# Seeding PSUM banks from ScalarE in the halved products of two feed-forward networks

## The chip, the core and the metric

The kernel runs on one core of a Trainium2 chip. A core has a matrix engine (TensorE, PE in the profile, its weight loads PEld), two engines for elementwise work (VectorE, DVE; ScalarE, ACT), a general engine (GpSimd, POOL) and a queue that issues transfers (SyncE, SP). They run beside each other and wait for each other through semaphores. TensorE writes only to PSUM, an on-chip memory used here as eight banks of 128 x 512 float32. The metric is the time on the device in microseconds (us), as the median of several executions; lower is better.

## The reference

One layer of a decoder on 512 tokens of 1024 features: a feed-forward network at half weight, a mixing stage (two kinds of attention, with gates), and a second feed-forward network at half weight. The change touches the two networks alone:

```python
def swiglu_ffn(x, g, w_gate, w_up, w_down):
    h = rms_norm(x, g)
    return (jax.nn.silu(h @ w_gate) * (h @ w_up)) @ w_down
```

`w_gate` and `w_up` are 1024 x 2816, that is 22 blocks of 128 columns, and `w_down` is 2816 x 1024. All is float32.

## The kernel before

**Numbers in two parts.** TensorE multiplies a rounded float32 format. Every operand is therefore split into a rounded part (`h`, `wh`, `ah`) and the remainder (`l`, `wl`, `al`), and each product is three matmuls: rounded by rounded, and the two mixed ones (`mm3`, lines 141 to 143). For weights, `split_w` casts on ScalarE (line 112) and subtracts on VectorE (line 117). For activations, `split_act` casts on ScalarE (line 212); the remainder comes either from a ScalarE negation (line 214) and a transfer issued by GpSimd that adds to its target (line 215), or, for the last pair of a group, from a VectorE difference (line 217).

**A network.** The 22 blocks are worked through in four groups: blocks 0 to 3 plainly, then three groups of six. After each group eight down steps (`run_down`) multiply the group's activations by its rows of `w_down` and add to x (line 419). The first two down steps put off the blocks that were finished last: each first does the others, and only then are the last two done, block 2q+1 ahead of block 2q.

**Pairs.** In the groups of six, blocks go in pairs (`pair_steps`), three pairs to a group, nine to a network, 18 in all. Gate and up of two blocks are a 2 x 2 product of halved matrices: features are halved, and tokens are halved to 256 columns. With Winograd's variant of Strassen's scheme it takes seven products of quarters instead of eight. The weights' quarters are a, b, c, d, with the sums s1 = c + d, s2 = s1 + a, s3 = c + a, s4 = s2 + b made on VectorE; the moving operands b1, b2, ta, tb are the quarters of the input and their sums, made once per network. A product is 24 matmuls (two halves for gate and up, four slices of features, three parts) into one bank. A bank can go on accumulating later, so several products are added up there; the banks A, B and C hold such sums, and what remains to be added is done by VectorE as it reads a bank out into `gu1` or `gu2`. `finish` then does Silu on ScalarE, the product with up on VectorE, and `split_act`.

**What sets the order.** TensorE's order is the order of the program. It runs a list of steps; ahead of step i, `look_ahead` emits the splits of weights up to step i+2 and the loads up to step i+6. There are three buffers for split weights, so the cast for step i+2 waits until TensorE has read the weights of step i-1. Raw quarters lie in five buffers; a step's last argument names those that come free after its split. The other engines' order is set by a planner, which runs the program against its own estimate of times, with dependencies and buffers. PSUM's eight banks are shared out by tag: three `acc`, two `s`, two `pt`, one `pv`. Before the change A, B and C are all `acc`; the down steps use `acc` too.

Of the kernel before, what the change touches and what calls it, by code (L numbers as in the profile page):

```python
# [11 lines left out]
F32 = mybir.dt.float32  # L12
F32R = mybir.dt.float32r
AF = mybir.ActivationFunctionType
OP = mybir.AluOpType
# [3 lines left out]
P = 128  # L19
T = 512  # L20
# [26 lines left out]
HT = T // 2  # L47
# [4 lines left out]
def tile_hybrid_layer(ctx: ExitStack, tc: tile.TileContext, a: dict):  # L52
    nc = tc.nc
    V, S, G, PE = nc.vector, nc.scalar, nc.gpsimd, nc.tensor
# [7 lines left out]
    psum = ctx.enter_context(tc.tile_pool(name="psum", bufs=1, space=PSUM))  # L62

    def acc_tile(name):
        return psum.tile([P, T], F32, tag="acc", bufs=3, name=name)

    def tmp_tile(name):
        return tmp.tile([P, T], F32, tag="t", name=name)
# [40 lines left out]
    def split_w(raw, f=1024, adding=False):  # L109
        wh = wpool.tile([P, 1088], F32R, tag="wh", name="wh")  # L110
        wl = wpool.tile([P, 1088], F32R, tag="wl", name="wl")
        S.copy(wh[:, :f], raw[:, :f])  # L112
        if adding:
            S.mul(wl[:, :f], wh[:, :f].bitcast(F32), -1.0)
            G.dma_start(wl[:, :f], raw[:, :f], accum_op=OP.add)
        else:
            V.tensor_sub(wl[:, :f], raw[:, :f], wh[:, :f].bitcast(F32))  # L117
        return wh[:, :1024], wl[:, :1024]
# [74 lines left out]
    def ffn(n, nxt, parts=lambda d: [slice(0, T)]):  # L193
        wg, wu, wp, wd = (a[f"w_{nm}{n}"] for nm in ("gate", "up", "pair", "down"))
        gi = 0 if n == 1 else 2
        with tc.tile_pool(name=f"ffn{n}", bufs=1) as ap, tc.tile_pool(name=f"halves{n}", bufs=1) as hp:
# [67 lines left out]
            def moving(nm, half):  # L264
                h, l = ops[nm]
                sl = slice(half * HT, half * HT + HT)
                return (h, l) if nm == "b1" else (h[:, :, sl], l[:, :, sl])
# [47 lines left out]
            def pair_steps(q, last):  # L315

                t, raw = {}, {}  # L320

                def view(ps):
                    return ps.rearrange("p (m t) -> p m t", m=2)

                def product(bank, w, b, start):
                    wh, wl = (z.rearrange("p (m k c) -> p m k c", m=2, k=HK) for z in w)
                    for m in range(2):
                        for k in range(HK):
                            mm3(bank[:, m * HT:(m + 1) * HT], wh[:, m, k], wl[:, m, k], b[0][:, k], b[1][:, k],
                                start and m == 0 and k == 0, m == 1 and k == HK - 1, skip_group_check=not start)  # L330

                def finish(f, gu):
                    S.activation(gu[:, 0], gu[:, 0], AF.Silu)
                    V.tensor_mul(gu[:, 1], gu[:, 1], gu[:, 0])
                    split_act(f, gu[:, 1], not last)

                def gu_tile():
                    return stream(2 + next(gu_at), F32, "gu").rearrange("p (m t) -> p m t", m=2)

                def split_a():  # L340
                    t["s1"] = stream(0, F32, "s1")
                    V.tensor_add(t["s1"], raw["c"][0], raw["d"][0])
                    return split_w(raw["a"][0])

                def split_s2():
                    t["s2"] = stream(1, F32, "s2")
                    V.tensor_add(t["s2"], t["s1"], raw["a"][0])
                    return split_w(t["s2"])

                def split_s3():  # L350
                    V.tensor_add(raw["c"][0], raw["c"][0], raw["a"][0])
                    return split_w(raw["c"][0])

                def split_s4():
                    V.tensor_add(t["s2"], t["s2"], raw["b"][0])
                    return split_w(t["s2"])

                def run_a(w):
                    t["A"] = acc_tile("pA")
                    product(t["A"], w, moving("b1", 0), True)  # L360
                    t["c1"] = tmp_tile("c1")
                    S.copy(t["c1"], t["A"])

                def run_s2(w):
                    t["B"] = acc_tile("pB")
                    product(t["B"], w, moving("tb", 0), True)
                    t["u2"] = tmp_tile("u2")
                    V.tensor_add(t["u2"], t["B"], t["c1"])

                def run_s1(w):  # L370
                    t["C"] = acc_tile("pC")
                    product(t["C"], w, moving("ta", 0), True)

                def run_s3(w):
                    product(t["B"], w, moving("ta", 1), False)
                    u3 = tmp_tile("u3")
                    V.tensor_add(u3, t["B"], t["c1"])
                    t["gu1"], t["gu2"] = gu_tile(), gu_tile()
                    V.scalar_tensor_tensor(t["gu2"][:, :, HT:], view(t["C"]), -1.0, view(u3), op0=OP.mult, op1=OP.subtract)

                def run_b(w):
                    product(t["A"], w, moving("b2", 0), False)
                    S.copy(t["gu1"][:, :, :HT], view(t["A"]))

                def run_d(w):
                    product(t["B"], w, moving("tb", 1), False)
                    V.scalar_tensor_tensor(t["gu2"][:, :, :HT], view(t["B"]), -1.0, view(t["c1"]), op0=OP.mult, op1=OP.subtract)
                    finish(2 * q + 1, t["gu2"])

                def run_s4(w):  # L390
                    product(t["C"], w, moving("b2", 1), False)
                    V.tensor_add(t["gu1"][:, :, HT:], view(t["C"]), view(t["u2"]))
                    finish(2 * q, t["gu1"])

                load = {z: (z, 0, wp[q - PLAIN // 2, i]) for i, z in enumerate("abcd")}
                return [Step(raw, [load["c"], load["d"], load["a"]], split_a, run_a),
                        Step(raw, [], split_s2, run_s2),
                        Step(raw, [load["b"]], lambda: split_w(t["s1"]), run_s1),
                        Step(raw, [], split_s3, run_s3, "ac"),
                        Step(raw, [], lambda: split_w(raw["b"][0]), run_b),  # L400
                        Step(raw, [], lambda: split_w(raw["d"][0]), run_d, "d"),
                        Step(raw, [], split_s4, run_s4, "b")]

            def run_down(d, lo, hi, held={}):

# [87 lines left out]
    with tc.tile_pool(name="begin", bufs=1) as bp, tc.manual_schedule(  # L493
# [3 lines left out]
        for d in range(KD):  # L497
            for dst, src, at in zip(first, ("w_gate1", "w_up1"), ({0: (0, 2), 2: (2, 8)}, {1: (0, 4), 4: (4, 8)})):
                if d in at:
                    lo, hi = at[d]  # L500
                    w = load_w(a[src][0][:, lo:hi], hi - lo, P, bp.tile([P, 1024], F32, name=f"raw{d}"))
# [18 lines left out]
    with (tc.tile_pool(name="mix", bufs=1) as mp, ExitStack() as att_ctx,  # L520
# [4 lines left out]
        tn, fv, iq, pA, ga, gb = {}, {}, [], [], [], []  # L525
# [246 lines left out]
        ps = transposed(lambda t: sd[1][:, t].rearrange("p a d -> p (a d)"), "ps_ik")  # L772
# [74 lines left out]
        for h in range(H):  # L847
# [3 lines left out]
            for i in range(1, NT):  # L851
                n = P * (i + 1)
                prod.run(FILL_IX)
                ps = psum.tile([P, T], F32, tag="s" if (h * 3 + i) % 2 else "pt", bufs=2, name="ps_ix")
# [156 lines left out]
        for g in range(2 * H):  # L1011
            q, k, bias = nq, nk, nb
# [31 lines left out]
        with tc.tile_pool(name="late", bufs=1) as lp:  # L1044
# [9 lines left out]
            ps = fm_product(load_w(a["w_gb"][7], KD, P), "ps_gb")  # L1054
# [6 lines left out]
            for d in range(KD):  # L1061
                wh, wl = load_w(a["w_bb"][d], 4, P)
                ps = acc_tile("ps_bb")
# [10 lines left out]
            for d in range(KD):  # L1074
                wh, wl = load_w(a["w_out"][d], KD, P)
                ps = acc_tile("ps_out")
# [86 lines left out]
```

## Time and profile before

| what | value |
| --- | --- |
| median of three executions | 1090.2 us (1090.1 to 1090.91) |
| the profiled execution: span from first to last instruction | 1087.8 us |
| TensorE matmuls, busy | 1071.0 us, 98% of the span |
| TensorE weight loads, busy | 963.3 us, 89% |
| VectorE busy | 791.2 us, 73% |
| ScalarE busy | 570.6 us, 52% |
| GpSimd busy | 197.6 us, 18% |
| read from memory | 104.94 MB |

Of the profiled execution the page gives the span; its time as the median counts it is not listed by itself, and the median lies 2.4 us above the span. A row of a group reads: line, engine, operation, output <- inputs, shapes, count, then busy time in us, the mean in ns of one, and the idle time of the engine just before, with what ended it. A row in order of time begins with start and duration in us. `x512` is a full bank, and one step's weights are `128x1024`. Matmuls overlap in the array, so the duration of one (279 ns for 256 columns) is longer than the distance between two.

### The profile page before, as it was taken

How to read it: one execution, taken by the hardware profiler on the slowest of the kernel's cores; microseconds unless marked ns; L12 is line 12 of the kernel's file. 1: busy time of each engine (PE TensorE's matmuls, PEld its weight loads, DVE VectorE, ACT ScalarE, POOL GpSimd, SP SyncE). 2: the span in 40 equal slices, each digit the busy share in tenths (PEclk: the TensorE clock that was granted, in tenths of full speed). 3: DMA queues.
4: the chain of work that ended last, by engine and by line, in shares of the span. 5: the costliest groups of instructions: out<-in, count | busy, mean ns of one | idle time of the engine just before them, and what ended most of it. 6: DMA issues, size and time to landing. Idle time of an engine off the chain costs nothing.

```text
span 1087.8 us, 17784 instructions
## 1 busy us (share of the span) xinstructions
PE 1071.0 (98%) x6808; PEld 963.3 (89%) x6808; DVE 791.2 (73%) x1286; ACT 570.6 (52%) x916; POOL 197.6 (18%) x265
## 2 busy tenths in 40 slices
PE   8999999999999999999999999999999999999998
PEld 6889989998998889999878788788889989989997
DVE  5888767856967579976776765954888758766963
ACT  6635533633555676467766656543635624533550
POOL 1100000100000014367786562000100000000000
PEclk9999999999999999999999999999999999999999
DMA  7554433443442258733323321533544442533441
GB/s 225 134 155 124 110 117 116 112 121 104 125 122 83 84 126 185 207 105 99 87 59 105 123 74 49 165 97 97 126 136 131 125 118 93 136 104 110 126 113 72
DMA packets 45444, 127.87 MB, mean 118 GB/s; under 512 B 5544, under 2 KB 5928, under 8 KB 45360
## 3 DMA queue, kind: packets, MB, share of 16 engines
q1 hardware_dynamic: 38880, 110.22, 33.1%
q0 software_dynamic: 6336, 16.26, 8.2%
q8 instruction: 54, 0.88, 0.3%
q10 hardware_dynamic: 144, 0.26, 0.1%
q14 instruction: 30, 0.25, 0.1%
HBM read 104.94 MB, written 3.42 MB: 100 GB/s over the span
## 4 chain that ended last, share of the span: by engine, by line
PE 53%; DVE 5%; ACT 3%; POOL 3%; issue 2%; DMA 0%; DVEq 0%; POOLq 0%; ACTq 0%
PE pd L142 4%; PE pd L143 4%; PE pd L141 4%; PE ps_f L141 3%; PE ps_f L142 3%; PE ps_f L143 3%; PE pB L142 2%; PE pB L141 2%; PE pB L143 2%; PE ps_t L141 2%; PE ps_t L142 2%; PE ps_t L143 2%; PE pC L142 2%; PE pA L142 2%; PE pA L141 2%
## 5 line engine op out<-in xcount | busy, mean ns | idle before, releaser
L142 PE MATMUL pd<-al,wh 128*128 128x512 f32 (+1 forms) x358 | 138.3, 386 | 1.0 <-DVE al L217 1.0
L141 PE MATMUL pd<-ah,wh 128*128 128x512 f32 (+1 forms) x358 | 138.2, 386 | 0.0
L143 PE MATMUL pd<-ah,wl 128*128 128x512 f32 (+1 forms) x358 | 138.0, 386 | 0.0
L215 POOL DMA_DIRECT2D al<-gu x24 | 20.5, 854 | 490.2 <-ACT al L214 490.2
L112 ACT CAST wh<-s 128x1024 fp32r<-128x1024 f32 x54 | 57.0, 1055 | 92.4 <-PE pB L142 45.9
L419 DVE SCALAR_TENSOR_TENSOR x<-pd,x 128x512 f32<-128x512 f32 (+1 forms) x65 | 44.2, 680 | 62.0 <-PE pd L143 61.8
L141 PE MATMUL ps_t<-wh,xh 128*128 128x256 f32 (+1 forms) x288 | 80.7, 280 | 0.0
L142 PEld LDWEIGHTS pd<-al,wh 128*128 128x128 f32 x358 | 67.2, 188 | 15.0 <-DVE al L217 1.7
L142 PE MATMUL ps_t<-wl,xh 128*128 128x256 f32 (+1 forms) x288 | 80.3, 279 | 0.0
L143 PE MATMUL pB<-tbh,wl 128*128 128x256 f32 x288 | 80.3, 279 | 0.0
L141 PE MATMUL pB<-tbh,wh 128*128 128x256 f32 x288 | 80.3, 279 | 0.0
L142 PE MATMUL pB<-tbl,wh 128*128 128x256 f32 x288 | 80.3, 279 | 0.0
L143 PE MATMUL ps_t<-wh,xl 128*128 128x256 f32 (+1 forms) x288 | 80.2, 279 | 0.0
L141 PEld LDWEIGHTS pd<-ah,wh 128*128 128x128 f32 x358 | 67.3, 188 | 13.6 <-ACT ah L212 0.3
L143 PEld LDWEIGHTS pd<-ah,wl 128*128 128x128 f32 x358 | 67.3, 188 | 13.4
L117 DVE TENSOR_TENSOR wl<-s,wh 128x1024 fp32r<-128x1024 f32 x54 | 65.8, 1218 | 4.2 <-ACT wh L112 3.8
L141 PE MATMUL ps_f<-xh,wh 128*128 128x512 f32 x152 | 60.5, 398 | 0.0
L143 PE MATMUL ps_f<-xh,wl 128*128 128x512 f32 x152 | 59.6, 392 | 0.0
L142 PE MATMUL ps_f<-xl,wh 128*128 128x512 f32 x152 | 59.6, 392 | 0.0
L112 ACT CAST wh<-re 128x1024 fp32r<-128x1024 f32 (+2 forms) x30 | 28.5, 951 | 55.4 <-PE pd L142 15.5
L112 ACT CAST wh<-ra 128x1024 fp32r<-128x1024 f32 (+2 forms) x32 | 29.8, 930 | 48.8 <-PE pd L142 18.7
L141 PEld LDWEIGHTS ps_t<-wh,xh 128*128 128x128 f32 x288 | 54.3, 189 | 0.5
(329 smaller groups left out, 3485.9 us busy)
## 6 DMA issues: line engine op xcount, KB each, us to landing
rb<-in_w_pair_dram SPq DMA_DIRECT2D x16, 512.0 KB, 3.7
re<-in_w_pair_dram SPq DMA_DIRECT2D x16, 512.0 KB, 3.7
rc<-in_w_pair_dram SPq DMA_DIRECT2D x14, 512.0 KB, 3.7
ra<-in_w_pair_dram SPq DMA_DIRECT2D x14, 512.0 KB, 3.6
rd<-in_w_pair_dram SPq DMA_DIRECT2D x12, 512.0 KB, 3.7
al<-gu POOLq DMA_DIRECT2D x24, 256.0 KB, 4.0
rd<-in_w_down_dram SPq DMA_DIRECT2D x12, 384.0 KB, 3.1
rc<-in_w_down_dram SPq DMA_DIRECT2D x10, 384.0 KB, 3.3
```

Of the source, the lines that this page charges most:

```text
L112: S.copy(wh[:, :f], raw[:, :f])
L117: V.tensor_sub(wl[:, :f], raw[:, :f], wh[:, :f].bitcast(F32))
L141: PE.matmul(out, lh, rh, start=start, stop=False, **more)
L142: PE.matmul(out, lh, rl, start=False, stop=False, **more)
L143: PE.matmul(out, ll, rh, start=False, stop=stop, **more)
L215: G.dma_start(l, u, accum_op=OP.add)
L419: V.scalar_tensor_tensor(x[d][:, cols], ps, 0.5, x[d][:, cols], op0=OP.mult, op1=OP.add)
```

## The change

In the pairs, a product that is needed in several sums is copied into the next bank by ScalarE before that bank's own products are added to it, where before it was copied to SBUF once and added by VectorE at each reading. A moves to a bank of tag `s`; s1's product gets a bank of its own (tag `pt`) and is copied to SBUF as p5. B starts from a copy of A, C from a copy of B after s2. VectorE's sums u2 and u3, and its negated difference at the end of d, go; the last becomes a ScalarE negation. The order of the seven steps a, s2, s1, s3, b, d, s4 becomes a, s1, s2, b, s3, s4, d. The load of quarter b hangs on the fourth step instead of the third, and the first half of a pair (block 2q) is now finished one step before the second (block 2q+1). `run_down` is as before.

```diff
+                def bank(tag, name):
+                    return psum.tile([P, T], F32, tag=tag, bufs=3 if tag == "acc" else 2, name=name)
+
                 def run_a(w):
-                    t["A"] = acc_tile("pA")
+                    t["A"] = bank("s", "pA")
                     product(t["A"], w, moving("b1", 0), True)
-                    t["c1"] = tmp_tile("c1")
-                    S.copy(t["c1"], t["A"])
+                    t["B"] = bank("acc", "pB")
+                    S.copy(t["B"], t["A"])
+
+                def run_s1(w):
+                    ps = bank("pt", "pD")
+                    product(ps, w, moving("ta", 0), True)
+                    t["p5"] = tmp_tile("p5")
+                    S.copy(t["p5"], ps)
 
                 def run_s2(w):
-                    t["B"] = acc_tile("pB")
-                    product(t["B"], w, moving("tb", 0), True)
-                    t["u2"] = tmp_tile("u2")
-                    V.tensor_add(t["u2"], t["B"], t["c1"])
-
-                def run_s1(w):
-                    t["C"] = acc_tile("pC")
-                    product(t["C"], w, moving("ta", 0), True)
+                    product(t["B"], w, moving("tb", 0), False)
+                    t["C"] = bank("acc", "pC")
+                    S.copy(t["C"], t["B"])
+
+                def run_b(w):
+                    product(t["A"], w, moving("b2", 0), False)
+                    t["gu1"], t["gu2"] = gu_tile(), gu_tile()
+                    S.copy(t["gu1"][:, :, :HT], view(t["A"]))
 
                 def run_s3(w):
                     product(t["B"], w, moving("ta", 1), False)
-                    u3 = tmp_tile("u3")
-                    V.tensor_add(u3, t["B"], t["c1"])
-                    t["gu1"], t["gu2"] = gu_tile(), gu_tile()
-                    V.scalar_tensor_tensor(t["gu2"][:, :, HT:], view(t["C"]), -1.0, view(u3), op0=OP.mult, op1=OP.subtract)
-
-                def run_b(w):
-                    product(t["A"], w, moving("b2", 0), False)
-                    S.copy(t["gu1"][:, :, :HT], view(t["A"]))
+                    V.scalar_tensor_tensor(t["gu2"][:, :, HT:], view(t["B"]), -1.0, view(t["p5"]), op0=OP.mult, op1=OP.subtract)
+
+                def run_s4(w):
+                    product(t["C"], w, moving("b2", 1), False)
+                    V.tensor_add(t["gu1"][:, :, HT:], view(t["C"]), view(t["p5"]))
+                    finish(2 * q, t["gu1"])
 
                 def run_d(w):
                     product(t["B"], w, moving("tb", 1), False)
-                    V.scalar_tensor_tensor(t["gu2"][:, :, :HT], view(t["B"]), -1.0, view(t["c1"]), op0=OP.mult, op1=OP.subtract)
+                    S.mul(t["gu2"][:, :, :HT], view(t["B"]), -1.0)
                     finish(2 * q + 1, t["gu2"])
-
-                def run_s4(w):
-                    product(t["C"], w, moving("b2", 1), False)
-                    V.tensor_add(t["gu1"][:, :, HT:], view(t["C"]), view(t["u2"]))
-                    finish(2 * q, t["gu1"])
...
                 return [Step(raw, [load["c"], load["d"], load["a"]], split_a, run_a),
+                        Step(raw, [], lambda: split_w(t["s1"]), run_s1),
                         Step(raw, [], split_s2, run_s2),
-                        Step(raw, [load["b"]], lambda: split_w(t["s1"]), run_s1),
+                        Step(raw, [load["b"]], lambda: split_w(raw["b"][0]), run_b),
                         Step(raw, [], split_s3, run_s3, "ac"),
-                        Step(raw, [], lambda: split_w(raw["b"][0]), run_b),
-                        Step(raw, [], lambda: split_w(raw["d"][0]), run_d, "d"),
-                        Step(raw, [], split_s4, run_s4, "b")]
+                        Step(raw, [], split_s4, run_s4, "b"),
+                        Step(raw, [], lambda: split_w(raw["d"][0]), run_d, "d")]
```

## The prediction, made before the changed kernel ran

> **What bounds the kernel now.** I read the page's totals first, then the busy time by stretches of time for the six stretches that hold the pairs, then the groups, the order of time on ScalarE and VectorE at two seams, and TensorE's waits.
>
> ```profile
> span 1087.8 us, 17784 instructions
> PE 1071.0 (98%) x6808; PEld 963.3 (89%) x6808; DVE 791.2 (73%) x1286; ACT 570.6 (52%) x916; POOL 197.6 (18%) x265
> ```
>
> TensorE works through 1071.0 of 1087.8 us; 16.8 us are left to gain anywhere. The pairs are 18 x 7 steps of 24 matmuls. Their stretches (three pairs each, six of them) read:
>
> ```profile
> core 0: us, PE busy (x) PEld busy (x) DVE busy (x) ACT busy (x) POOL busy (x), PEclk, DMA share, GB/s
> 78.75:137.55 58.80, 58.80 (x505) 58.76 (x504) 47.52 (x50) 31.94 (x41) 3.39 (x4) 1.00 0.43 118
> ...
> 992.70:1051.50 58.80, 58.80 (x505) 58.76 (x504) 46.55 (x49) 32.06 (x41) 3.44 (x4) 1.00 0.43 112
> sum 352.80, PE 352.80 PEld 352.55 DVE 280.84 ACT 191.87 POOL 20.49; mean PE 58.80 PEld 58.76 DVE 46.81 ACT 31.98 POOL 3.42
> ```
>
> The reader is to see two things. Matmuls overlap, so a busy PE alone could hide slack; but the weight loads, one for each matmul, are busy for 352.55 of 352.80 us too. And VectorE, which the change relieves, stands idle for 72 of these 353 us without TensorE waiting once. That the pace is even is seen in the first and last starts of one tile:
>
> ```profile
> L141 PE MATMUL pA<-b1h,wh x144: 277/278/283, 79.0 to 1034.5; 128*128 128x256 f32 x144
> L141 PE MATMUL pA<-b2h,wh x144: 277/279/281, 90.2 to 1045.7; 128*128 128x256 f32 x144
> ...
> L362 ACT COPY c<-pA x18: 572/582/584, 82.8 to 1035.9; 128x512 f32<-128x512 f32 x18
> L368 DVE TENSOR_TENSOR u<-pB,c x18: 690/692/692, 84.8 to 1037.9; 128x512 f32<-128x512 f32 x18
> L377 DVE TENSOR_TENSOR u<-pB,c x18: 681/683/692, 91.2 to 1043.5; 128x512 f32<-128x512 f32 x18
> L387 DVE SCALAR_TENSOR_TENSOR gu<-pB,c x18: 679/691/692, 96.0 to 1049.1; 128x512 f32<-128x512 f32 x18
> ```
>
> From a to b are four steps: 90.2 - 79.0 = 11.2 in the first pair, 1045.7 - 1034.5 = 11.2 in the last, 2.80 us a step in both. So seven steps cost 19.6 us, and no relief of another engine makes them shorter.
>
> **The change, part by part.** *Products.* Still seven of 24 matmuls each, in another order: 0.
>
> *VectorE.* Removed per pair: u2 (0.692), u3 (0.683) and the negated difference in d (0.691), 2.07 us, or 37 us in 18 pairs. What stays is the sum of s3 and that of s4 with p5. All of it lies beside saturated TensorE: worth 0 on the path.
>
> *ScalarE.* c1's copy becomes B's seed; new are p5's copy, C's seed and the negation, three operations of 128x512 read from PSUM. p5's copy is c1's operation, 0.58 us by L362's row. No row shows ScalarE writing PSUM. The nearest rows bound a seed and the negation: a scaling cast of this size and an operation on one column.
>
> ```profile
> L152 ACT ACTIVATE xh<-x,gains 128x512 fp32r<-128x512 f32 x24 | 17.2, 719 | 2.0 <-DMA x<-in_x_dram 1.4 <-DMA gains<-in_gains_dram 0.2
> ...
> L877 ACT ACTIVATION_READ_ACCUMULATOR p<-p,mn 128x1 f32 x64 | 12.0, 188 | 0.0
> ```
>
> So 0.19 to 0.72 us; I take 0.58, since L362's copy is nearest (same source, same size). That is 1.74 us more per pair on an engine that works 32 of 58.8 us per three pairs: beside other work, if no TensorE step waits for it.
>
> *The new waits.* s2 needs B seeded, that is the copy of A after a; s1 lies between, 2.80 us. s4 needs C seeded, the copy after s2; b and s3 lie between, 5.6 us. b must not write A, nor s3 B, before those copies have read them: one step or more between. d must not write B before VectorE has read it after s3; s4 lies between. Tightest is B's seed, at the seam of two pairs, where ScalarE also finishes the pair before:
>
> ```profile
> 98.69 1.06 ACT L112 CAST wh<-s 128x1024 fp32r<-128x1024 f32 x1 [1.23 <-PE pC L142]
> ...
> 101.44 1.05 ACT L112 CAST wh<-rd 128x1024 fp32r<-128x1024 f32 x1
> 102.39 0.58 ACT L362 COPY c<-pA 128x512 f32<-128x512 f32 x1
> 102.87 0.63 ACT L212 CAST ah<-gu 128x512 fp32r<-128x512 f32 x1
> 103.52 0.64 ACT L214 ACTIVATE al<-ah 128x512 fp32r<-128x512 f32 x1
> 104.24 1.05 ACT L112 CAST wh<-rc 128x1024 fp32r<-128x1024 f32 x1
> ```
>
> The weight casts (wh) mark the steps: each starts about 0.1 us into one, so here a runs from 98.55 to 101.35 and the second step to 104.15. ScalarE is full in these two: from 98.69 to 104.24 eight operations follow each other without a pause (left out are the cast ah, the remainder al and a Silu), 5.55 of 5.60 us. The same list stands there afterwards with gu1 and gu2 swapped, plus the negation, which takes 0.48 (102.39 to 102.87) of issue. If the whole 0.5 comes ahead of the seed, it ends at 102.97 + 0.5 = 103.47; s2 starts at 104.15. Left over: 0.7 us, 1.2 where the negation falls into an idle moment. With 0.72 for each of negation and seed the rest is still 0.4; with 0.19, above 1.4. So no wait. What is late next is the cast at 104.24, by up to 0.45 us, and VectorE behind it:
>
> ```profile
> 105.32 1.22 DVE L117 TENSOR_TENSOR wl<-rc,wh 128x1024 fp32r<-128x1024 f32 x1 [0.21 <-ACT wh L112]
> ```
>
> That difference ends at 106.54, for a step that starts two later, at 109.75: 3.2 us of cover against 0.45. Cost 0; were the cover gone, 0.45 us at each of 12 seams (two within each of six groups), 5.4 us.
>
> *Loads.* The fourth quarter (b) is asked for one step later and used one later; c and a come free one step later, since s3 is now fifth; s1, whose sum needs c and d, is now second. SyncE's queue does nothing but loads. Its present times:
>
> ```profile
> 84.17 0.33 SPq L468 DMA_DIRECT2D rb<-in_w_pair_dram  x1
> ...
> 87.63 1.23 DVE L342 TENSOR_TENSOR s<-rd,rb 128x1024 f32<-128x1024 f32 x1 [0.69 <-DMA rb<-in_w_pair_dram]
> ```
>
> The load that the next pair's s1 waits for goes out at 84.17 and has landed 3.46 us later. One step later is 86.97, the sum 90.4 to 91.7. s1 will start at 101.35, its cast two steps ahead, at 95.8: 4 us of cover. VectorE stands in order behind such a sum as it does now (0.69), with 3.2 us of cover for each difference. Cost 0.
>
> *The seam from pairs to the down projections.* The last pair's two halves now end in the other order: gu1 (2q) after s4, gu2 (2q+1) after d. The down step's order is not changed: it puts off the last two, and takes 2q+1 first.
>
> ```profile
> 137.75 0.39 PE L141 MATMUL pd<-ah,wh 128*128 128x512 f32 x1
> ...
> 143.22 0.39 PE L141 MATMUL pd<-ah,wh 128*128 128x512 f32 x1
> ```
>
> and on ScalarE and VectorE beside it:
>
> ```profile
> 138.02 0.83 ACT L112 CAST wh<-rd 128x768 fp32r<-128x768 f32 x1
> 138.76 0.63 ACT L333 ACTIVATE gu<-gu 128x512 f32<-128x512 f32 x1
> ...
> 139.16 0.95 DVE L117 TENSOR_TENSOR wl<-rd,wh 128x768 fp32r<-128x768 f32 x1
> 140.03 0.68 DVE L334 TENSOR_TENSOR gu<-gu 128x512 f32<-128x512 f32 x1
> 141.40 0.69 DVE L217 TENSOR_TENSOR al<-gu,ah 128x512 fp32r<-128x512 f32 x1 [0.69 <-ACT ah L212]
> ```
>
> Let T = 137.75, the first down matmul. The put-off part starts after 24 matmuls, at T+5.47. Now the half that ends last is ready at 142.09, T+4.34, and read one set of three matmuls after T+5.47, at about T+6.15: 1.8 us spare. Afterwards: cast to T+1.0, negation to T+1.6, Silu to T+2.25, product behind VectorE's wl (which ends at T+2.3 as now) to T+3.0, cast to T+3.6, difference to T+4.35, as late as now, since the negation fits before wl is done. It is read at T+5.47 (cast) and T+5.70 (difference): 1.35 us spare. The second down bank may be the one that the negation frees, at T+1.6; it is first written at T+2.73. Cost 0.
>
> *Sum.* 0 + 0 + 0 + 0 = 0 on a span of 1087.8 us. The median shown is 1090.2, so 2.4 us lie around the span; forecast **1090.2 us**. A change below 0.2% (2.2 us) is one that a measurement of this kernel cannot tell from none.
>
> **Rivals.**
>
> *A, the seed comes late (slower).* One mechanism: at the 12 seams ScalarE's queue holds the finished half's cast and its remainder (ah, al) ahead of the seed, instead of behind the copy as at 102.39 to 103.52. The seed then ends 0.65 + 0.53 later than 103.47, at 104.65 to 104.9 with its own issue, and TensorE, with nothing but s2 next in its queue, waits 0.5 to 0.75 us. It decides once more than 0.7 us stands ahead of the seed. Twelve times 0.7 is 8.4: **1098.6 us**. For it: ScalarE full in 5.55 of 5.60 us. Against: Silu of the late half must come after the negation, so its product on VectorE cannot be much earlier than now, and ah is ready no sooner.
>
> *B, the down seam (slower).* gu2's chain falls more than 1.35 us behind, by one full weight difference (1.22) and a cast (0.83) more ahead of it: 2.05 - 1.35 = 0.7 us at six seams, 4.2 us: **1094.4 us**. For it: TensorE's waits show that this very place has stalled, though in the plain group only:
>
> ```profile
> PE pd L142 <- DVE al L217: 1.0, 2, 0.7
> ```
>
> Against: fewer VectorE operations stand there than now.
>
> *C, the mixing stage is planned anew (either way).* The order on all engines but TensorE comes from the planner's own run of the program, and the banks and buffers that the first network leaves are others. The mixing stage is where TensorE does wait; by stretches of time, with the columns as above:
>
> ```profile
> 360.00:706.00 346.00, 337.69 (x2065) 296.71 (x2065) 262.26 (x637) 225.67 (x461) 164.51 (x217) 1.00 0.40 113
> ```
>
> It idles 8.3 us there. A third of it moved is 2.8 us: **1087.4** or **1093.0 us**. This is the only way to faster that I see.
>
> *D, the clock.* If waits for seeds made the granted clock fall to half for a step at each seam, 12 x 2.8 = 33.6 us: **1123.8 us**. Against: from 360 to 706 TensorE idles 8.3 us in all and the granted clock stays 1.00. The Trainium skill (TensorE: Matmul & The Clock Gate, "A second HAM failure mode: psum-queue depth-cycling") describes a kernel that cycled PSUM banks and idled in small pieces until its clock swung between half and full; by that rule D would be likely, and the trace does not bear it out, with its clock of 1.00 from 360 to 706 beside 8.3 us of idling.
>
> **How the numbers follow.** Forecast (no wait, same) 0.74; A 0.08; B 0.04; C faster 0.08, C slower 0.05; D 0.01. Faster 0.08, same 0.74, slower 0.08 + 0.04 + 0.05 + 0.01 = 0.18. The range goes from 1088.2 (part of C's faster side) over B and C's slower side to 1096.5 (A with 0.5 us a seam); outside stay most of A, D and the far half of C faster, some 0.13.
>
> **What would show it.** Right: each step of the pairs still 2.80 us, the pairs' stretches still 58.80 of 58.80 us on TensorE with VectorE down by about 6 us in each (three times 2.07) and ScalarE up by about 5; no wait of pB or pC on ScalarE. Each part has its own row: the seeds' duration near 0.58; the seed's end before s2's first matmul; the down seam without a wait on al. Wrong: waits of TensorE on pB's or pC's seed at the seams (A), on ah or al at the down seams (B), or an idle sum in the mixing stage away from 8.3 us (C).

## The result and the profile after

| kernel | median | runs |
| --- | --- | --- |
| before | 1090.56 us | 4 (1090.1 to 1091.45) |
| changed | 1101.7 us | 4 (1099.49 to 1102.78) |

The ratio is 1.0103, with a 95% interval of 1.0089 to 1.0118: the changed kernel is slower by 1%, some 11 us. The forecast was 1090.2 us, in a range up to 1096.5. The prediction was wrong.

The page's totals of the changed kernel:

```profile
span 1099.3 us, 17737 instructions
PE 1076.2 (98%) x6808; PEld 966.2 (88%) x6808; DVE 758.3 (69%) x1232; ACT 595.2 (54%) x970; POOL 200.9 (18%) x265
```

The work moved as described: VectorE does 33 us less (791.2 before), ScalarE 25 us more, with the same 6808 matmuls. The span grew by 11.5 us all the same. The busy time by stretches, cut as in the prediction (first matmul of a to first down matmul, columns as there), says where:

```profile
79.21:139.51 60.30, 59.29 (x506) 58.94 (x504) 42.73 (x42) 35.62 (x49) 3.40 (x4) 1.00 0.45 117
172.17:232.62 60.45, 59.47 (x505) 59.12 (x504) 42.72 (x42) 35.63 (x49) 3.40 (x4) 1.00 0.41 109
265.30:325.81 60.51, 59.28 (x506) 58.93 (x504) 42.72 (x42) 35.60 (x49) 3.40 (x4) 1.00 0.41 110
816.81:877.34 60.53, 59.29 (x506) 58.94 (x505) 42.88 (x43) 35.61 (x49) 3.44 (x4) 1.00 0.42 118
...
sum 362.15, PE 355.93 PEld 353.84 DVE 256.52 ACT 213.73 POOL 20.53; mean PE 59.32 PEld 58.97 DVE 42.75 ACT 35.62 POOL 3.42
```

The six stretches take 362.15 us instead of 352.80, so 9.35 of the 11.5 us lie in the pairs. Before, a weight load was busy in practically all of a stretch; now 362.15 - 353.84 = 8.3 us have none. TensorE's waits name what for (engine, tile, line, what was waited for: us in total, times, longest):

```profile
PE pB L141 <- DVE gu L385: 5.2, 11, 1.0
...
PE pB L141 <- ACT wh L112: 1.0, 1, 1.0
...
PE pd L142 <- DVE al L217: 0.9, 2, 0.7
```

Line 385 is VectorE's read of bank B after s3, which makes half of gu2. TensorE waits for it with the first matmul of d, which writes B again. The one wait that is put down to a weight cast (line 112) is of the same kind: there (third group, second pair) VectorE's read ended at 303.18, and d's first matmul started at 303.33, the same 0.15 behind it as at the first seam below. The listed idle time begins only where the matmul before has ended, 0.28 us after its start, while matmuls otherwise start every 0.12 us; so the price is better read from starts. In order of time, first pair and second pair of the first group, the first matmul of s4 and the first of d:

```profile
93.21 0.28 PE L141 MATMUL pC<-b2h,wh 128*128 128x256 f32 x1
...
96.39 0.36 PE L141 MATMUL pB<-tbh,wh 128*128 128x256 f32 x1 [0.21 <-DVE gu L385]
...
113.27 0.28 PE L141 MATMUL pC<-b2h,wh 128*128 128x256 f32 x1
...
117.03 0.36 PE L141 MATMUL pB<-tbh,wh 128*128 128x256 f32 x1 [0.80 <-DVE gu L385]
```

A step takes 2.80 us, so d should start at 96.01 and 116.07; it is 0.38 and 0.96 us late. In all six groups the first pair's d is late by 0.38 to 0.51 and the second's by 0.56 to 1.17, 8.14 us together; the step after each such wait takes some 0.08 more, about 1 us in twelve. That is 9.1 of the 9.35; nearly all of the rest is the third pair of the second group, which ran at 2.827 us a step without a wait. The third pair of a group, which no pair follows, has no such wait.

VectorE in order of time, at the first seam:

```profile
90.88 1.23 DVE L342 TENSOR_TENSOR s<-rd,rb 128x1024 f32<-128x1024 f32 x1 [0.83 <-DMA rb<-in_w_pair_dram]
92.14 1.22 DVE L347 TENSOR_TENSOR s<-s,re 128x1024 f32<-128x1024 f32 x1
93.29 1.22 DVE L117 TENSOR_TENSOR wl<-rc,wh 128x1024 fp32r<-128x1024 f32 x1
94.42 1.22 DVE L351 TENSOR_TENSOR rd<-rd,re 128x1024 f32<-128x1024 f32 x1
95.56 0.68 DVE L385 SCALAR_TENSOR_TENSOR gu<-pB,p 128x512 f32<-128x512 f32 x1
```

The bank has been complete since s3 ended at 93.21. But the read is fifth in a row. First comes the sum s1 of the *next* pair, which waits for a load; behind it, in order, the next pair's s2, a split, and the next pair's sum for s3; each takes some 1.14 us from start to start. The read ends at 96.24, and d follows 0.15 later.

VectorE at the same place in the kernel before:

```profile
88.89 1.23 DVE L351 TENSOR_TENSOR rd<-rd,re 128x1024 f32<-128x1024 f32 x1
90.03 1.22 DVE L117 TENSOR_TENSOR wl<-rc,wh 128x1024 fp32r<-128x1024 f32 x1
91.17 0.68 DVE L377 TENSOR_TENSOR u<-pB,c 128x512 f32<-128x512 f32 x1
...
93.50 1.21 DVE L347 TENSOR_TENSOR s<-s,re 128x1024 f32<-128x1024 f32 x1
```

There too the read of B (line 377) stood behind the late sum (87.63, in the prediction's rows), but only three operations deep, with the next pair's s2 (line 347) after it. It ended at 91.85. TensorE's first matmul of d there:

```profile
92.95 0.28 PE L141 MATMUL pB<-tbh,wh 128*128 128x256 f32 x1
```

So 1.10 us were spare. Now the bill at the first seam. The load goes out at 87.23 instead of 84.17, as d comes one step later too; measured back from d's due start, the sum begins 96.01 - 90.88 = 5.13 us ahead instead of 92.95 - 87.63 = 5.32, so 0.19 is lost. The fourth operation costs 1.14. 1.10 - 0.19 - 1.14 = -0.23, and 0.15 from the read's end to the matmul make 0.38. At the second seam the load itself takes longer from issue to use, 107.32 to 111.65, 4.33 us against 3.39 before (103.77 to 107.16), and that makes its wait the longer one. SyncE's queue of the changed kernel:

```profile
107.32 0.33 SPq L470 DMA_DIRECT2D rd<-in_w_pair_dram  x1
```

and on VectorE:

```profile
111.65 1.23 DVE L342 TENSOR_TENSOR s<-ra,rd 128x1024 f32<-128x1024 f32 x1 [1.59 <-DMA rd<-in_w_pair_dram]
...
116.20 0.68 DVE L385 SCALAR_TENSOR_TENSOR gu<-pB,p 128x512 f32<-128x512 f32 x1
```

Of the 2.15 us of span outside the pairs, 1.63 lie between the third stretch and the fourth (491.00 us, against 489.37 in early_release below). There, in the mixing stage, the granted clock stood at half for a while (columns as before):

```profile
441.00:443.00 2.00, 2.00 (x7) 1.52 (x5) 2.00 (x7) 0.00 (x0) 1.03 (x1) 0.50 0.84 158
```

The clock is 0.90 in the 2 us ahead of this row and 0.75 in the 2 us behind it, so it stood at half for 3.4 us in all; in them matmuls of 512 columns start every 0.43 us (441.29, 441.72, 442.14) instead of every 0.23. Half of 3.4 is 1.7 us lost. It isn't the change's: the profiled execution of load_held_2, an experiment below that has none of the change and takes what the kernel before takes, shows the same. What brings it on isn't shown.

```profile
435.00:437.00 2.00, 2.00 (x6) 1.59 (x5) 2.00 (x8) 0.09 (x1) 1.87 (x2) 0.50 0.38 74
```

### The profile page after: what moved, and what is told of

Its sections match the earlier page's. It is cut to its first block, busy times and chain, and to the rows that moved or that the text cites. A ratio compares the mean times of both kernels' runs of the same rounds, so it can differ in the third digit from the quotient of the medians.

```text
span 1099.3 us, 17737 instructions
## 1 busy us (share of the span) xinstructions
PE 1076.2 (98%) x6808; PEld 966.2 (88%) x6808; DVE 758.3 (69%) x1232; ACT 595.2 (54%) x970; POOL 200.9 (18%) x265
## 4 chain that ended last, share of the span: by engine, by line
PE 48%; DVE 7%; ACT 5%; POOL 3%; issue 2%; DMA 2%; DVEq 0%; POOLq 0%; ACTq 0%
PE pd L142 4%; PE pd L143 4%; PE pd L141 4%; PE ps_f L141 3%; PE ps_f L142 3%; PE ps_f L143 3%; PE ps_t L141 2%; PE ps_t L143 2%; PE ps_t L142 2%; PE pB L141 2%; PE pB L142 2%; PE pB L143 2%; PE ps_out L142 1%; PE pt L888 1%; PE ps_out L143 1%
## 5 line engine op out<-in xcount | busy, mean ns | idle before, releaser
L141 PEld LDWEIGHTS pB<-tbh,wh 128*128 128x128 f32 x288 | 54.1, 188 | 8.3 <-issue 8.3
```

What stands on the lines that cost most here:

```text
L141: PE.matmul(out, lh, rh, start=start, stop=False, **more)
```

## The experiments

**Theory 1.** The price is the wait of d for VectorE's read of B; the cause is the block of sums for the next pair that stands ahead of it in VectorE's order and starts late, because c and a are released late. The first rival: the seeds and the negation on ScalarE, or the added waits as such, slow TensorE. The second rival: the late release and load are bad by themselves, whatever stands behind them.

### Release c and a earlier

early_release is the changed kernel, with the sum for s3 formed two steps sooner in the buffer of s1, which is free by then:

```diff
 def split_s2():
     t["s2"] = stream(1, F32, "s2")
     V.tensor_add(t["s2"], t["s1"], raw["a"][0])
+    V.tensor_add(t["s1"], raw["c"][0], raw["a"][0])
     return split_w(t["s2"])
 def split_s3():
-    V.tensor_add(raw["c"][0], raw["c"][0], raw["a"][0])
-    return split_w(raw["c"][0])
+    return split_w(t["s1"])
...
-    Step(raw, [], split_s2, run_s2),
+    Step(raw, [], split_s2, run_s2, "ac"),
...
-    Step(raw, [], split_s3, run_s3, "ac"),
+    Step(raw, [], split_s3, run_s3),
```

> Edit to the changed kernel: the sum s3 = c + a is formed together with s2, in the buffer of s1, so that the raw quarters c and a come free with the third step's split instead of the fifth's; nothing else moves, no operation is added. Theory 1 (late loads: the next pair's sums stand on VectorE ahead of the read of B after s3, and wait for a load that goes out one step later than before): the loads go out two steps earlier, the sums are through before s3 ends, d starts at once; the 9 us of waits before d go, 1091 to 1093 us. Rival (the planner's order alone puts the sums ahead of the read, whenever the loads land): as the changed kernel, 1099 to 1102 us. Rival (ScalarE's seeds and their traffic in PSUM slow the pairs): 1099 to 1102 us.

Measured: 1090.52 us, 0.9995 (0.9986 to 1.0004) of the kernel before. All of the loss is gone, seeds and negation kept. Its stretches:

```profile
261.91:320.71 58.80, 58.80 (x505) 58.80 (x504) 43.54 (x42) 35.41 (x49) 3.40 (x4) 1.00 0.43 122
810.08:868.88 58.80, 58.80 (x506) 58.80 (x504) 44.18 (x43) 35.41 (x49) 3.44 (x4) 1.00 0.41 122
...
sum 352.82, PE 352.82 PEld 352.80 DVE 262.53 ACT 212.48 POOL 20.54; mean PE 58.80 PEld 58.80 DVE 43.75 ACT 35.41 POOL 3.42
```

VectorE at the first seam:

```profile
87.06 1.23 DVE L342 TENSOR_TENSOR s<-rd,rb 128x1024 f32<-128x1024 f32 x1
...
93.18 0.69 DVE L385 SCALAR_TENSOR_TENSOR gu<-pB,p 128x512 f32<-128x512 f32 x1 [0.60 <-PE pB L143]
```

The sum of the next pair no longer waits for a load, and the read now waits for TensorE's s3 itself: it is as early as it can be. The first rival falls, and the new order of the seven steps, which is kept too, can't be the cause by itself; theory 1 and the second rival stand.

### Late release in the kernel before

late_release is the kernel before with the list that hands c and a back one step later:

```diff
-    Step(raw, [], split_s3, run_s3, "ac"),
-    Step(raw, [], lambda: split_w(raw["b"][0]), run_b),
+    Step(raw, [], split_s3, run_s3),
+    Step(raw, [], lambda: split_w(raw["b"][0]), run_b, "ac"),
```

> Edit to the kernel before: quarters c and a are given free one step later (with the split of b, fifth, instead of that of s3, fourth); no seeds, the old order, no operation added. Theory 1 (late loads): the next pair's sums come 2.8 us later and meet the reads of B and C; TensorE waits at some seams, 1094 to 1100 us. Rival (the seeds, or the new order of the seven): no change, 1090 to 1091 us.

Measured: 1091.33 us, 0.9997 (0.9987 to 1.0006). It decides nothing. The load still went out at 83.81: the list only sets when a buffer is handed out, and the transfer waits for the buffer's last reader, which had not moved.

### Sums behind the read

sums_behind_read is the changed kernel with only an order: the next pair's s1 may be queued on VectorE no earlier than the read of B. Loads stay late.

```diff
+    with tc.issue_after(read_b[0].ins) if read_b[0] else nullcontext():
-    V.tensor_add(t["s1"], raw["c"][0], raw["d"][0])
+        V.tensor_add(t["s1"], raw["c"][0], raw["d"][0])
...
-    V.scalar_tensor_tensor(t["gu2"][:, :, HT:], view(t["B"]), -1.0, view(t["p5"]), ...
+    read_b[0] = V.scalar_tensor_tensor(t["gu2"][:, :, HT:], view(t["B"]), -1.0, view(t["p5"]), ...
```

> Edit to the changed kernel: the first of the next pair's sums (s1) is queued on VectorE behind the read of B after s3; loads, seeds and steps stay. Theory 1 in its narrow form (the wait is VectorE's in-order queue: sums that wait for a load stand ahead of the read): TensorE's wait before d goes although the loads stay late, 1091 to 1094 us; the sums then start after s3, about 3 us later, and the casts behind them may take up to 0.5 us at some seams. Rival (late loads hurt in themselves, through the next pair's weights): TensorE waits at the next pair's first steps instead, 1097 to 1102 us. Rival (seeds): 1099 to 1102 us.

Measured: 1090.6 us, 0.9996 (0.9988 to 1.0005); the stretches are 58.80 again. VectorE at the first seam:

```profile
93.42 0.69 DVE L386 SCALAR_TENSOR_TENSOR gu<-pB,p 128x512 f32<-128x512 f32 x1 [0.61 <-PE pB L143]
94.03 1.22 DVE L343 TENSOR_TENSOR s<-rd,rb 128x1024 f32<-128x1024 f32 x1
```

The read comes at s3's end, and the sums start at 94.03, three us later than in the changed kernel, with no harm to anyone. The loads are as late as in the changed kernel (the one for this sum goes out at 87.24, there at 87.23); the order alone takes the loss away.

### The read without VectorE

b_read_by_scalar does not touch VectorE's order by its edit, but ScalarE copies B out, so that d waits for ScalarE:

```diff
-    V.scalar_tensor_tensor(t["gu2"][:, :, HT:], view(t["B"]), -1.0, view(t["p5"]), ...
+    u3 = tmp_tile("u3")
+    S.copy(u3, t["B"])
+    V.scalar_tensor_tensor(t["gu2"][:, :, HT:], view(u3), -1.0, view(t["p5"]), ...
```

> Edit to the changed kernel: after s3 ScalarE copies B to SBUF and VectorE's difference reads that copy, so that d waits for ScalarE's copy and not for VectorE; one copy of 0.58 us more per pair on ScalarE, loads and order as changed. Theory 1: the copy ends about 1.6 us after s3, within the 2.8 us of s4; no wait before d, 1091 to 1093 us. Rival (late loads hurt through the next pair's weights): 1097 to 1102 us. Rival (ScalarE is the cause): slower still, above 1102 us.

Measured: 1090.96 us, 0.9993 (0.9983 to 1.0002). ScalarE's copy at the first seam:

```profile
93.97 0.58 ACT L386 COPY u<-pB 128x512 f32<-128x512 f32 x1
```

and VectorE there:

```profile
90.30 1.22 DVE L342 TENSOR_TENSOR s<-rd,rb 128x1024 f32<-128x1024 f32 x1 [0.54 <-DMA rb<-in_w_pair_dram]
...
96.11 0.69 DVE L387 SCALAR_TENSOR_TENSOR gu<-u,p 128x512 f32<-128x512 f32 x1
```

VectorE still waits for the load and does its part at 96.11, behind five operations now (the planner put one split more ahead), later than in the changed kernel, and no step of TensorE is late for it. What hurt was that a PSUM bank's release hung on it.

### A seed without cover

The seeds cost nothing as placed. What would they cost with no step between? seed_uncovered is sums_behind_read with s2 directly behind a:

```diff
     Step(raw, [load["c"], load["d"], load["a"]], split_a, run_a),
-    Step(raw, [], lambda: split_w(t["s1"]), run_s1),
     Step(raw, [], split_s2, run_s2),
+    Step(raw, [], lambda: split_w(t["s1"]), run_s1),
```

> Edit to the kernel with the sums behind the read: s2 follows directly on a, s1 comes after it, so that no product lies between A's last matmul and the first that adds to the seeded B. It measures what the seed's wait costs where nothing covers it. Theory (a seed is a plain copy, hidden by one product of 2.8 us): s2 waits for the weight cast (0.95) and the seed (0.58), about 1.6 to 1.7 us in each of 18 pairs, 29 to 31 us: 1119 to 1122 us. Rival (PSUM to PSUM is cheap, or the seed goes ahead of the cast): 0.7 us in each pair, 13 us, 1103 to 1105 us. Rival (seeds disturb the matmuls themselves): more than 31 us, with steps longer than 2.80 us.

Measured: 1123.45 us, 1.0302 (1.0285 to 1.0319). TensorE's waits, and then ScalarE in the first pair:

```profile
PE pB L141 <- ACT pB L366: 27.1, 18, 1.5
```

```profile
82.27 1.04 ACT L112 CAST wh<-ra 128x1024 fp32r<-128x1024 f32 x1 [1.86 <-PE pA L142]
83.22 0.58 ACT L366 COPY pB<-pA 128x512 f32<-128x512 f32 x1
```

All 18 pairs now wait. From a's first matmul (79.38) to s2's (83.85) it is 4.47 us, 1.67 over a step: the seed stands behind a weight cast and then takes its 0.58. The stretches sum to 385.59, 32.8 over those of the kernel before, more than the 29 to 31 expected. The waits are as expected, 18 x 1.67 = 30.1; the step behind each takes another 0.11 to 0.14 (2.1 together), and in five third pairs the other steps ran at 2.827 us (0.7). The rival that seeds disturb the matmuls themselves doesn't follow from this: in sums_behind_read the same 36 seeds leave every step at 2.80. That cover of one step, which the prediction relied on, is real.

### A longer block

block_longer is the changed kernel with the sum s1 made twice, one operation more on VectorE:

```diff
     V.tensor_add(t["s1"], raw["c"][0], raw["d"][0])
+    V.tensor_add(t["s1"], raw["c"][0], raw["d"][0])
```

> Edit to the changed kernel: the first of the next pair's sums (s1 = c + d) is made twice, 1.14 us more on VectorE per pair. In the order that the planner now sets, this adds one operation ahead of the read of B after s3 in a group's first pair, and in its second pair it takes the place of the sum s3, which goes behind the read. Theory (the wait before d is what stands ahead of the read on VectorE, counted from the load's landing): the wait of the first seams grows from 0.4 by 1.14 to about 1.5 us, that of the second stays near 1.0; 6 x 1.14 = 6.8 us more, 1107 to 1110 us. Rival (the wait is set by something else than the queue's length, by the load alone or by ScalarE): as the changed kernel, 1099 to 1103 us.

Measured: 1101.69 us, 1.0106 (1.009 to 1.0121), short of the 1107 to 1110 expected. The first seam did as expected, with five operations ahead of the read: d came 96.46 - 92.29 = 4.17 us after s4, so 1.37 late instead of 0.38. At the second seam the order was planned anew, as VectorE shows:

```profile
111.07 1.23 DVE L342 TENSOR_TENSOR s<-ra,rd 128x1024 f32<-128x1024 f32 x1 [0.94 <-DMA rd<-in_w_pair_dram]
112.21 1.22 DVE L117 TENSOR_TENSOR wl<-rb,wh 128x1024 fp32r<-128x1024 f32 x1
113.34 1.22 DVE L343 TENSOR_TENSOR s<-ra,rd 128x1024 f32<-128x1024 f32 x1
114.48 0.68 DVE L386 SCALAR_TENSOR_TENSOR gu<-pB,p 128x512 f32<-128x512 f32 x1
```

Only three stand ahead there (the doubled sum among them), the read ends at 115.16, and s4 ends at 116.14: no wait, though the load is late. In five of the six groups the second seam has none. My expectation took the order as given, which it isn't. That makes a series: three operations behind a late load leave 0.98 us, four cost 0.38 (first seam of the changed kernel), five 1.37, with the sum beginning 5.07, 5.13 and 5.27 us ahead of d's due start. The lateness is much the same in all three, so here it is the depth of the block that decides. It is not the depth alone: at the second seam of the third group three operations stand ahead too, but the sum began only 3.69 us ahead of d's due start (298.71 against 302.40), and d came 0.55 late.

### A late load alone

load_held was to try the second rival by itself: the kernel before, with a VectorE operation on one column that reads c with b's split and so really holds the buffer a step longer.

```diff
+def split_b():
+    w = split_w(raw["b"][0])
+    hold = small.tile([P, 1], F32, tag="hold", name="hold")
+    V.tensor_add(hold, raw["c"][0][:, 0:1], w[1][:, 0:1].bitcast(F32))
+    return w
```

> Edit to the kernel before: a VectorE operation on one column reads quarter c together with the split of b, so that c's buffer really comes free one step later and the next pair's load goes out 2.8 us later, as in the changed kernel; old order, no seeds. The planner's own order then has the sums of the next pair behind both sums that read B and C. Theory (a late load costs only what stands behind it on VectorE): no wait in the pairs, 1090 to 1092 us. Rival (a late load is bad in itself, through the next pair's weights): waits at each next pair's first steps, 1096 us or more.

Measured: 1102.86 us, 1.0113 (1.0097 to 1.0128), which looks like that rival. But no matmul of the pairs waits. Every step is longer, 2.848 us in five of the groups and 2.816 in the sixth instead of 2.800, and the down matmuls too. The new tile of one column had moved the activations and the halved operands up by 128 bytes in each partition. Two runs separate the two: load_held_2 writes the column into a buffer that exists already, and tiles_moved_128 only adds the unused small tiles.

```diff
-    hold = small.tile([P, 1], F32, tag="hold", name="hold")
-    V.tensor_add(hold, raw["c"][0][:, 0:1], w[1][:, 0:1].bitcast(F32))
+    hold = tmp_tile("hold")
+    V.tensor_add(hold[:, 0:1], raw["c"][0][:, 0:1], w[1][:, 0:1].bitcast(F32))
```

> The same edit to the kernel before as in load_held (quarter c read once more, on one column, together with the split of b, so that the next pair's load goes out one step later), but the column is written into a buffer that exists, so that no tile of the networks moves. In load_held the added small tile moved the activations and halved operands by 128 bytes in each partition, and TensorE's pace was 2.85 us a step with no wait. Theory (a late load costs only what stands behind it on VectorE, and the sums stand behind the reads here): steps of 2.80 us, no wait in the pairs, 1090 to 1092 us. Rival (the late load slows the pairs): 2.85 us a step again, 1100 to 1104 us.

> Edit to the kernel before: one small tile more (four buffers of one column, cleared at the start, read by nobody), which moves the activations and the halved operands by 128 bytes in each partition; loads, order and work as before. Theory (the pace in load_held came from the operands' place alone): about 2.85 us a step in the pairs and 232 ns between the down matmuls, 1100 to 1104 us. Rival (it came from the held load): 2.80 us a step, 1090 to 1091 us.

Measured: load_held_2 1090.86 us, 1.0003 (0.9994 to 1.0013); tiles_moved_128 1102.35 us, 1.0106 (1.0091 to 1.0121). The place alone explains load_held. And the late load alone, in load_held_2, costs nothing: it goes out at 87.33, and the order that was planned with it puts both reads ahead of the sum. VectorE at the first seam:

```profile
90.34 0.69 DVE L383 TENSOR_TENSOR u<-pB,c 128x512 f32<-128x512 f32 x1 [0.61 <-PE pB L143]
91.06 0.69 DVE L385 SCALAR_TENSOR_TENSOR gu<-pC,u 128x512 f32<-128x512 f32 x1
...
92.80 1.22 DVE L342 TENSOR_TENSOR s<-rd,rb 128x1024 f32<-128x1024 f32 x1
```

The second rival falls, and theory 1 is narrower than I put it. Counted back from d's due start, the load goes out 8.78 us ahead both before (92.95 - 84.17) and after the change (96.01 - 87.23): it was late before, too. What is new is the fourth operation behind it and ahead of a bank's read; why the planner put it there, no run shows. Either end of that chain can be cut, the lateness (early_release) or the order (sums_behind_read).

### Places in SBUF

tiles_moved_32 adds one unused tile of one column, which moves the same tiles by 32 bytes (the raw buffers rd and re lie with the activations, so they move too). It belongs with the two above.

> The same with one buffer, which moves those tiles by 32 bytes. Theory (the place of the moving operand against the weights sets the pace): no number from the runs so far for 32 bytes; between the kernel before and the 128 byte move, 1090 to 1104 us. Rival (the place does not matter): 1090 to 1091 us.

Measured: 1091.64 us, 1.0012 (1.0002 to 1.0022), with unexpected stretches:

```profile
78.62:137.99 59.37, 59.37 (x506) 59.37 (x505) 47.14 (x50) 32.15 (x41) 3.40 (x4) 1.00 0.43 117
171.57:228.69 57.12, 57.12 (x505) 57.12 (x504) 46.38 (x49) 32.09 (x41) 3.39 (x4) 1.00 0.43 116
...
sum 347.21, PE 347.21 PEld 347.19 DVE 279.33 ACT 192.68 POOL 20.49; mean PE 57.87 PEld 57.87 DVE 46.56 ACT 32.11 POOL 3.41
```

Four of six stretches are *shorter* than in any kernel so far, 57.12 us, 2.72 a step; 5.6 us are gained in the pairs. They are lost again in the down projections. Between two stretches lie 144 down matmuls; from 137.99 to 171.57 it is 33.58 us, where the changed kernel has 172.17 - 139.51 = 32.66. That is 6.4 ns for each; 1056 of them (two networks, eight steps, 22 blocks, three parts) make 6.7 us. 6.7 - 5.6 = 1.1, against 1.3 by the measured ratio.

Could one have the one without the other? The down matmuls read the activations, the pairs' matmuls the halved operands. The last two kernels move the halved operands alone by those 32 bytes, in the kernel before and in early_release:

```diff
-            hp.tile([P, 8], F32, name="pad")
+            hp.tile([P, 16], F32, name="pad")
```

> The kernel before with its unused tile pad 16 columns wide instead of 8, which moves the halved operands by 32 bytes in each partition and leaves the activations where they were. If the place of the halved operands alone sets the pace of the pairs (as in tiles_moved_32, where the activations moved as well): a step of 2.72 us in four of the six groups and 2.83 in two, stretches of 57.1 and 59.4 us, down matmuls at 226.7 ns again, and a time of 1084 to 1086 us. If the pace needs the activations to move too: stretches of 58.8 and 1090 to 1091 us.

> The same move of 32 bytes in the changed kernel with its sums made early (early_release, which took what the kernel before took). By the place of the halved operands: the same stretches as in halves_moved_before, 1084 to 1086 us, and no wait of d. If the shorter step takes away cover: 0.08 us less for each wait of a step, so none of over 0.3 us should come. By the rival: 1090 to 1091 us.

Measured: 1094.48 us, 1.003 (1.0017 to 1.0043), and 1094.52 us, 1.0031 (1.002 to 1.0042). Neither expectation holds. The stretches of halves_moved_before:

```profile
79.39:138.76 59.37, 59.37 (x506) 59.36 (x505) 47.25 (x50) 32.18 (x41) 3.39 (x4) 1.00 0.43 119
171.43:230.80 59.37, 59.37 (x506) 59.36 (x505) 46.52 (x49) 32.17 (x41) 3.39 (x4) 1.00 0.41 112
...
sum 356.21, PE 356.21 PEld 356.17 DVE 280.84 ACT 193.10 POOL 20.48; mean PE 59.37 PEld 59.36 DVE 46.81 ACT 32.18 POOL 3.41
```

The down matmuls keep their pace (171.43 - 138.76 = 32.67), as expected, but all six stretches take 59.37, 3.4 us more, which is the whole loss. So a move of the halved operands alone does change the pace of the pairs; the short step of 2.72 needs something more, which also differs between the groups of one network. No kernel here beats the kernel before.

## Why the prediction was wrong

**The step that failed** is "d must not write B before VectorE has read it after s3; s4 lies between". The wait was listed, and never priced. It was checked that a step lies between, and not when VectorE comes to the read. The rows to price it were in the trace of before: the read (line 377) stood three operations behind a sum that waits for a load, and ended 1.10 us ahead of d. That is a cover smaller than one VectorE operation, and it is this cover that one more operation used up.

**Its other half** is under *Loads*: "VectorE stands in order behind such a sum as it does now (0.69), with 3.2 us of cover for each difference. Cost 0." The lateness was right: one step was forecast, and the load went out 3.06 us later, 0.26 of which is the changed kernel's later start. The landing was forecast as of before, and came 0.19 us later at the first seam and 0.94 at the second. The cover of the weights was right too: no split is late in the runs where the loads stay late and the read goes first. But of what stands behind the sum only the weights' differences were looked at, not the read of a bank. And "as it does now" took the order as kept, where the planner put the next pair's s2 ahead of the read.

**The rivals.** A, the seed late at 12 seams, gave 1098.6 and was nearest in time, with another cause. The twelve seams were the right place, but no seed is waited for there. The second pair's seed and the first matmul of s2, in order of time:

```profile
103.29 0.58 ACT L365 COPY pB<-pA 128x512 f32<-128x512 f32 x1
...
104.87 0.28 PE L141 MATMUL pB<-tbh,wh 128*128 128x256 f32 x1
```

The seed ends 1.0 us ahead of s2, where 0.7 to 1.2 was forecast. B (down seam) didn't come: line 217's wait is 0.9 us in two, 1.0 before. The second half's product there,

```profile
141.81 0.69 DVE L334 TENSOR_TENSOR gu<-gu 128x512 f32<-128x512 f32 x1 [0.20 <-ACT gu L333]
```

ends 2.99 us after the first down matmul (139.51), against a forecast of T+3.0. C: what a new order of the mixing stage is worth can't be told beside its 3.4 us at half clock here; early_release, whose order is new there too, takes the time of before. D: the clock is 1.00 in every stretch of the pairs, with 8 us of small waits among them, and it is 1.00 in those of seed_uncovered with its 27.1 us of waits. So the rule that the prediction drew from the Trainium skill (TensorE: Matmul & The Clock Gate, "A second HAM failure mode: psum-queue depth-cycling") is not borne out in the pairs either. That the clock can fall to half in this kernel the mixing stage shows, 3.4 us of it, in kernels with and without the seeds.

**Right:** a seed at 0.58 us and hidden; no wait of pB or pC on ScalarE's copies; no wait at the down seam; 2.80 us a step elsewhere, but for the one pair at 2.827; and that VectorE's relief is worth nothing, with its 33 us on the page for the 37 forecast. In the stretches the shifts were mis-sized, VectorE by 4.06 us a stretch (46.81 to 42.75) for "about 6" and ScalarE by 3.64 (31.98 to 35.62) for "about 5"; nothing hung on them. Nor did anything hang on the range's upper end: A with 0.5 us a seam gives 1090.2 + 12 x 0.5 = 1096.2, where 1096.5 was put. That "no relief of another engine makes them shorter" held in every run, but 2.80 isn't a floor, as the places in SBUF show.

## What to carry to other kernels

Price every wait that a bank's reuse adds from the *reader's* queue: find in the trace when the reading engine comes to that instruction, and what stands ahead of it, above all an operation that itself waits for a load. An idle share of 30% on an in-order engine is no cover, and the cover of a listed wait is not the steps between on TensorE, but the time from the read's end to the next write. Where such a read is short of time, queue it ahead of work for later steps (sums_behind_read), or give back buffers sooner (early_release); and when a kernel changes pace without any wait, look at where its operands lie before blaming an edit.

## What the runs showed of the hardware

The distance between matmuls changed with where operands lie in SBUF, by moves of 32 and of 128 bytes. A step of 24 matmuls took 2.72, 2.80, 2.816, 2.827 or 2.848 us with no wait, at a granted clock of 1.00. A move of 128 bytes (tiles_moved_128):

```profile
79.75:139.56 59.81, 59.81 (x505) 59.80 (x504) 47.19 (x50) 32.16 (x41) 3.40 (x4) 1.00 0.43 117
173.03:232.84 59.81, 59.81 (x505) 59.80 (x504) 46.58 (x49) 32.19 (x41) 3.39 (x4) 1.00 0.42 111
```

Down matmuls take 32.66 / 144 = 227 ns in one placing, 33.47 / 144 = 232 in this, 33.58 / 144 = 233 in tiles_moved_32. Which operands must lie how was not found, and the place is not all: the pairs' pace also changed between groups of one run, and with all tiles in place it went to 2.827 in one pair of the changed kernel, three of block_longer, five of seed_uncovered and one of b_read_by_scalar. Each time it set in behind a wait of TensorE (in b_read_by_scalar one of 0.03 us, for a seed that ended at 306.63 where s2 started at 306.68) and lasted to the next wait or to the group's end; most waits left 2.80. In all these stretches the weight loads are busy practically throughout, at 57.12 us as at 59.81. The Trainium skill (Perfetto Trace Analysis, "Identifying the Most-Contended Engine") judges TensorE's headroom by its share of peak FLOPs and by that busy share. Here the busy share was full in stretches of 58.80, and stretches of 57.12 were still to be had, so a full share was no floor.
